# Column mean of an 8192 x 8192 matrix: loads of two rows per partition, a PSUM bank of its own for the last column block, and wider last pieces

## The chip, the cores and the metric

The kernel runs on one core of a Trainium2 chip; the other cores are idle. The metric is the device time of one execution in microseconds (us). The median of three runs of the kernel before is 634.28 us (634.18 to 634.52). "Span" is the time that the profile covers, about 1.8 us less than the device time.

## The reference

```python
def setup_inputs():
    return {"x": np.random.randn(8192, 8192).astype(np.float32)}

def reference(x):
    return np.mean(x, axis=0)
```

The input has 268.4 MB and the output 32 KB. Every input byte is needed once, so the kernel is a stream of loads with a little arithmetic behind it.

## The kernel before

128 rows at a time go into SBUF (the core's buffer for tiles), one row per partition. TensorE sums over the partitions with a constant 128x32 weight of 1/8192. The 16 blocks of 512 columns go to four banks of PSUM (the memory that TensorE accumulates into), four 32-partition quadrants each, and accumulate over all rows.

```python
    banks = [psp.tile([P, F], f32, name=f"bank{b}") for b in range(NB)]   # F = 512, NB = 4
    for ri in range(n_rt - 1):                     # 63 tiles of 128 rows, five buffers
        t = ld.tile([P, N], f32)
        nc.sync.dma_start(out=t[:], in_=x[ri * P:(ri + 1) * P, :])
        for b in range(NB):
            for q in range(4):
                c = (b * 4 + q) * F
                mm(b, q, 0, F, t[:, c:c + F], ri == 0, False)
    # ... the last 128 rows: three pieces of four blocks, then four pieces of
    # 128 columns of each of the last four blocks (runs of 512 bytes)
    for s in range(F // SPL):                      # SPL = 128
        t = lastp.tile([P, 4, SPL], f32, name=f"lasts{s}")
        nc.sync.dma_start(out=t[:], in_=x_v[r0:r0 + P, b, :, s * SPL:(s + 1) * SPL])
        for q in range(4):
            mm(b, q, s * SPL, SPL, t[:, q, :], False, s == F // SPL - 1)
    nc.vector.tensor_copy(out=r[:], in_=banks[b][:])
    nc.scalar.dma_start(out=out_v[b], in_=r[0:128:32, :])
```

Of the kernel before, what the change touches and what calls it, by code (L numbers as in the profile page):

```python
# [1 line left out]

# [4 lines left out]


@with_exitstack
def kernel(  # L10
    ctx: ExitStack,
    tc: tile.TileContext,
    x: bass.AP,
    out: bass.AP,
):







    nc = tc.nc
    f32 = mybir.dt.float32
    M, N = x.shape
    P = nc.NUM_PARTITIONS
    F = 512
    NB = N // (4 * F)
    n_rt = M // P
    SPL = 128  # L30

    ld = ctx.enter_context(tc.tile_pool(name="ld", bufs=5))
    lastp = ctx.enter_context(tc.tile_pool(name="lastp", bufs=1))
    sg = ctx.enter_context(tc.tile_pool(name="sg", bufs=1))
    psp = ctx.enter_context(tc.tile_pool(name="psum", bufs=1, space=bass.MemoryType.PSUM))
    resp = ctx.enter_context(tc.tile_pool(name="res", bufs=1))

    ones = sg.tile([P, 32], f32)
    nc.vector.memset(ones[:], 1.0 / M)  # L39
    banks = [psp.tile([P, F], f32, name=f"bank{b}") for b in range(NB)]  # L40

    def mm(b, q, c0, w, rhs, start, stop):
        nc.tensor.matmul(  # L43
            out=banks[b][32 * q:32 * q + 32, c0:c0 + w],
            lhsT=ones[:],
            rhs=rhs,
            start=start,
            stop=stop,
            tile_position=(0, 32 * q),
            skip_group_check=True,  # L50
        )

    for ri in range(n_rt - 1):
        t = ld.tile([P, N], f32)
        nc.sync.dma_start(out=t[:], in_=x[ri * P:(ri + 1) * P, :])  # L55
        for b in range(NB):
            for q in range(4):
                c = (b * 4 + q) * F
                mm(b, q, 0, F, t[:, c:c + F], ri == 0, False)

    r0 = (n_rt - 1) * P
    out_v = out.rearrange("(b q c) -> b q c", b=NB, q=4)
    x_v = x.rearrange("r (b q c) -> r b q c", b=NB, q=4)
    for b in range(NB - 1):
        t = lastp.tile([P, 4, F], f32, name=f"last{b}")
        nc.sync.dma_start(out=t[:], in_=x_v[r0:r0 + P, b])
        for q in range(4):
            mm(b, q, 0, F, t[:, q, :], False, True)
        r = resp.tile([P, F], f32, name=f"r{b}")
        nc.vector.tensor_copy(out=r[:], in_=banks[b][:])  # L70
        nc.scalar.dma_start(out=out_v[b], in_=r[0:128:32, :])
    b = NB - 1
    r = resp.tile([P, F], f32, name=f"r{b}")
    for s in range(F // SPL):
        t = lastp.tile([P, 4, SPL], f32, name=f"lasts{s}")
        nc.sync.dma_start(out=t[:], in_=x_v[r0:r0 + P, b, :, s * SPL:(s + 1) * SPL])  # L76
        for q in range(4):
            mm(b, q, s * SPL, SPL, t[:, q, :], False, s == F // SPL - 1)
    nc.vector.tensor_copy(out=r[:], in_=banks[b][:])  # L79
    nc.scalar.dma_start(out=out_v[b], in_=r[0:128:32, :])  # L80


# [1 line left out]
_INS = ['x']  # L84
_OUTS = [((8192,), 'float32')]


# [23 lines left out]
```

## Time and profile before

| What | Value |
|---|---|
| Time, median | 634.28 us |
| Span | 632.6 us |
| TensorE busy | 57% |
| Load rate, 100 to 600 us | 431 GB/s |
| Last landing of input data | 628.78 us |
| From there to the end of the span | 3.8 us |

The landing of a tile is seen in the timeline: TensorE's first matmul of a tile starts when the tile has landed. The trace also holds the semaphore updates of each load, 16 for a tile, which I take as one from each of the 16 DMA engines. The matmul at 43.54 us starts 0.04 us after the last of its 16, so the slowest engine sets the landing. These are landings of the kernel before near the start (columns: start us, busy us, engine, line, operation, count, and in brackets the idle time before and what ended it):

```profile
32.47 5.95 PE L43 MATMUL bank<-t,ones 128*32 128x512 f32 x32 [4.38 <-DMA t<-in_x_dram]
43.54 5.54 PE L43 MATMUL bank<-t,ones 128*32 128x512 f32 x32 [5.12 <-DMA t<-in_x_dram]
53.27 5.34 PE L43 MATMUL bank<-t,ones 128*32 128x512 f32 x32 [4.18 <-DMA t<-in_x_dram]
```

The last interval is 9.73 us, the usual one. The one before is 11.07 us. A "step" is from here on an interval between landings that is about 1.0 to 1.5 us longer than the usual one.

### The profile page before, as it was taken

The numbers are of one execution on the slowest core, as the hardware profiler recorded it, in microseconds if no ns is written. First come the engines' busy times: TensorE is split into PE (matmuls) and PEld (weight loads), VectorE is DVE, ScalarE is ACT, GpSimd is POOL, SyncE is SP. The second block draws the span as 40 slices with busy tenths as digits, with TensorE's granted clock in tenths as the row PEclk, the third lists the DMA queues.
The fourth block names the chain that finished last, engine by engine and source line by source line (L and its number), as shares of the span: only waits on it lengthen the run. The fifth ranks groups of instructions, "written<-read, shape, count | busy, mean of one in ns | idle before, by whom it ended". The sixth has DMA issues, their size and how long they took to land.

```text
span 632.6 us, 4331 instructions
## 1 busy us (share of the span) xinstructions
PE 363.6 (57%) x2072; PEld 82.7 (13%) x2072; DVE 2.9 (0%) x5; POOL 0.2 (0%) x4
## 2 busy tenths in 40 slices
PE   1564754656547546565476554655646646556466
PEld 0111111111111111111111111111111101111111
DVE  0000000000000000000000000000000000000001
POOL 0000000000000000000000000000000000000000
PEclk9868668667786686677866778668766686687767
DMA  9999999999999999999999999999999999999996
GB/s 371 433 440 437 432 431 431 428 431 430 431 433 430 431 430 433 431 432 431 430 431 431 428 434 430 431 431 430 433 428 431 431 430 431 432 435 430 431 427 233
DMA packets 11665, 268.74 MB, mean 425 GB/s; under 512 B 1136, under 2 KB 3184, under 8 KB 3200
## 3 DMA queue, kind: packets, MB, share of 16 engines
q1 hardware_dynamic: 11616, 268.44, 99.0%
q8 instruction: 16, 0.26, 0.2%
q10 hardware_dynamic: 32, 0.03, 0.0%
q14 instruction: 1, 0.01, 0.0%
HBM read 268.44 MB, written 0.03 MB: 424 GB/s over the span
## 4 chain that ended last, share of the span: by engine, by line
DMA 87%; PE 11%; SPq 1%; issue 0%; DVE 0%
DMA t<-in_x_dram 86%; PE bank L43 11%; DMA lasts<-in_x_dram 1%; SPq L76 1%; SPq L55 0%; DVE r L79 0%
## 5 line engine op out<-in xcount | busy, mean ns | idle before, releaser
L43 PE MATMUL bank<-t,ones 128*32 128x512 f32 x2016 | 359.8, 880 | 265.1 <-DMA t<-in_x_dram 265.1
L43 PEld LDWEIGHTS bank<-t,ones 128*32 128x32 f32 x2016 | 81.2, 153 | 542.5 <-DMA t<-in_x_dram 310.8
L70 DVE COPY r<-bank 128x512 f32<-128x512 f32 x3 | 2.1, 692 | 625.3 <-PE bank L43 625.3
L43 PE MATMUL bank<-last,ones 128*32 128x512 f32 x24 | 2.7, 592 | 0.0
L43 PE MATMUL bank<-lasts,ones 128*32 128x128 f32 x32 | 1.5, 279 | 0.5 <-DMA lasts<-in_x_dram 0.5
L43 PEld LDWEIGHTS bank<-last,ones 128*32 128x32 f32 x24 | 0.7, 110 | 2.2 <-issue 1.9
L43 PEld LDWEIGHTS bank<-lasts,ones 128*32 128x32 f32 x32 | 0.8, 109 | 1.6 <-DMA lasts<-in_x_dram 1.3
L79 DVE COPY r<-bank 128x512 f32<-128x512 f32 x1 | 0.7, 692 | 1.1 <-PE bank L43 1.1
L95 POOL MEMSET const-bfloat16-1.0<- 128x1 bf16 x1 | 0.1, 102 | 0.0
L95 POOL MEMSET const-uint8-127<- 128x1 uint8 x1 | 0.1, 102 | 0.0
L95 POOL MEMSET const-float32-0.0<- 128x1 f32 x1 | 0.1, 99 | 0.2 <-issue 0.2
L95 POOL MEMSET const-float32-1.0<- 128x1 f32 x1 | 0.1, 99 | 0.0
L39 DVE MEMSET ones<- 128x32 f32 x1 | 0.1, 85 | 0.8 <-PEq L95 0.8
## 6 DMA issues: line engine op xcount, KB each, us to landing
t<-in_x_dram SPq DMA_DIRECT2D x63, 4096.0 KB, 43.1
last<-in_x_dram SPq DMA_DIRECT2D x3, 1024.0 KB, 45.3
lasts<-in_x_dram SPq DMA_DIRECT2D x4, 256.0 KB, 19.1
out_dram<-r ACTq DMA_DIRECT2D x4, 8.0 KB
```

The costliest lines, as they stand in the source:

```text
L39: nc.vector.memset(ones[:], 1.0 / M)
L43: nc.tensor.matmul(out=banks[b][32 * q:32 * q + 32, c0:c0 + w], lhsT=ones[:], rhs=rhs, start=start, stop=stop, tile_position=(0, 32 * q), ...
L70: nc.vector.tensor_copy(out=r[:], in_=banks[b][:])
L76: nc.sync.dma_start(out=t[:], in_=x_v[r0:r0 + P, b, :, s * SPL:(s + 1) * SPL])
L79: nc.vector.tensor_copy(out=r[:], in_=banks[b][:])
L95: nc = _bacc.Bacc("TRN2", target_bir_lowering=False, num_devices=1)
```

## The change

Its intent is to cut the fixed cost of packets with runs twice as long, and to end with fewer and wider pieces, while the last block is spread over four quadrants of its own bank so that its matmuls and its copy stay short.

```diff
+    J = 2
+    NBLK = N // F - 1
+    W = F // 4
+    xt = x.rearrange("(t p j) c -> t p j c", p=P, j=J)
-    ld = ctx.enter_context(tc.tile_pool(name="ld", bufs=5))
+    ld = ctx.enter_context(tc.tile_pool(name="ld", bufs=3))
+    edge = psp.tile([P, W], f32, name="edge")
...
+    def sums(t, j, blocks, first, last):
+        for i in blocks:
+            if i < NBLK:
+                mm(banks[i // 4], i % 4, t[:, j, i * F:(i + 1) * F], first, last)
+            else:
+                for q in range(4):
+                    c = i * F + q * W
+                    mm(edge, q, t[:, j, c:c + W], first, last)
...
+    for ti in range(n_t - 1):
+        t = ld.tile([P, J, N], f32)
+        nc.sync.dma_start(out=t[:], in_=xt[ti])
+        for j in range(J):
+            sums(t, j, range(NBLK + 1), ti == 0 and j == 0, False)
+    t = ld.tile([P, J, N], f32)
+    cuts = [(0, 8), (8, 12), (12, 15), (15, 16)]
... (each piece: load, sums, copy of its banks, store on the scalar queue)
```

## The prediction

> **What bounds the kernel now.** I read the page first: the span, the busy shares, the slices and the chain that ended last.
>
> ```profile
> span 632.6 us, 4331 instructions
> PE 363.6 (57%) x2072; PEld 82.7 (13%) x2072; DVE 2.9 (0%) x5; POOL 0.2 (0%) x4
> ...
> DMA  9999999999999999999999999999999999999996
> ...
> DMA t<-in_x_dram 86%; PE bank L43 11%; DMA lasts<-in_x_dram 1%; SPq L76 1%; SPq L55 0%; DVE r L79 0%
> ```
>
> The DMA engines are full in every slice but the last, and TensorE is idle 43% of the time. The "PE bank L43 11%" in the chain is no TensorE bound: it is the step "a buffer was released, so a load was issued", and each such load then waits some 43 us in the queue behind its predecessors. The kernel is a 268.4 MB load stream with a head and a tail. Next I asked the DMA view for the steady stretch from 100 to 600 us.
>
> ```profile
> DMA packets 7404, 215.58 MB, mean 431 GB/s; under 512 B 818, under 2 KB 818, under 8 KB 818
> ...
> q1 hardware_dynamic: 7390, 215.35, 100.1%
> q8 instruction: 13, 0.21, 0.2%
> ```
>
> 215.35 MB is 6572 packets of 32 KB; the other 818 are 4-byte semaphore writes. 100.1% of 16 engines for 500 us is 8008 us, so a packet with its share of semaphore writes costs 1218 ns. So one row of x is one packet. Queue q8 is TensorE's instruction stream, 16 KB at a time, and it takes turns on the same engines.
>
> Then the end, in the chain in order of time, and the engines' load in the same microseconds (window, us, the busy columns, clock, DMA share, GB/s).
>
> ```profile
> 618.32 3.74 SPq L76
> 622.06 0.04 issue
> 622.10 6.68 DMA lasts<-in_x_dram
> 628.78 0.04 issue
> 628.83 0.47 PE bank L43 x8
> 629.30 0.02 issue
> 629.32 0.69 DVE r L79
> ```
>
> ```profile
> 622.00:624.00 2.00, 2.00 (x12) 0.40 (x8) 0.00 (x0) 0.00 (x0) 0.50 1.06 345
> 625.00:626.00 1.00, 1.00 (x12) 0.24 (x8) 0.16 (x1) 0.00 (x0) 1.00 0.77 221
> 627.00:628.00 1.00, 0.92 (x24) 0.34 (x13) 0.83 (x2) 0.00 (x0) 1.00 0.55 165
> ```
>
> The last landing is at 628.78; matmuls, copy and store take 3.8 us more. Before it the DMA share falls to 0.55: about half of the engines are done while the slow ones finish.
>
> **What the Trainium skill says.** "DMA: Bandwidth & Descriptors", section "Where 436 GB/s comes from": 16 ports x 32 B x 850 MHz, 435.2 GB/s. The packet records of this trace agree. The fastest 32 KB packet took 1213 ns and the fastest 8 KB packet 309 ns; the difference, 904 ns for 24,576 B, is 27.19 GB/s per engine, or 435 GB/s for 16. Same page, "Why small descriptors are slow (HBM only)": a fixed overhead of about 3 cycles per packet. The trace shows a larger one: 309 - 8192/27.19 = 7.7 ns, 6.5 cycles of 850 MHz. The 512 B packets fit (18.8 + 7.7 = 26.5; their median is 27 ns). Same page, "Latency and other measured facts": row pitches at large powers of two slow copies (207 GB/s at 512 KiB pitch, 103 at 4 MiB). The pitch between partitions here goes from 32 to 64 KB; no run here shows harm yet. "TensorE: Matmul & The Clock Gate", Part 1: half clock after an idle window of about 3.4 us, full clock after as long a busy one. The trace agrees: TensorE idles 3.4 to 4.4 us before each tile and then runs at 0.50 from 618 to 624 us, 0.85 us for four 512-wide matmuls, and later 0.43 us.
>
> **The change, part by part.** My working formula for a packet of n bytes is 7.7 ns + n/27.19.
>
> (a) *Two rows per partition.* 63 loads of 4 MB become 31 of 8 MB. If the two rows go as one 64 KB packet, 4 MB on one engine costs 4 x (2410 + 7.7) ns + half a 9 ns semaphore write = 9.676 us; now it is 8 x 1213 + 9 = 9.713 us, and the trace's tiles do land every 9.71 or 9.72 us. That is 0.037 us per 4 MB, over 62 such units 2.3 us. If the descriptor generator cuts the run at 32 KB, only the semaphore writes go: 0.0045 x 62 = 0.3 us. I can't tell which from the trace (its largest packet is 32 KB); I give the whole run 0.6. The mean packet is 5 ns above the fastest; I take that extra as per byte, so unchanged.
>
> (b) *Three buffers of 64 KB for five of 32 KB.* A buffer comes free about 9 to 10 us after its tile lands (twice the present 5 to 6.5 us, less the second half's cold clock). A tile takes 19.4 us to stream, so the next load joins the queue with about 29 us of loads ahead of it (before: 4 x 9.7 - 6 = 33). No starvation, 0 us.
>
> (c) *The last pieces.* At present each engine's last 4 MB is 24 packets of 8 KB (7.4 us) and 128 of 512 B (3.5 us), 10.9 us. The real interval between the last full tile (618.35) and the last landing (628.78) is 10.4. The new last 8 MB is 16 packets each of 16, 8, 6 and 2 KB: 16 x (610 + 309 + 234 + 83) = 19.8 us, against 9.7 + 10.9 = 20.6. So 0.8 us is saved. The stall of 3.74 us at L76 (semaphores shared with earlier loads) goes too, but the slow engines were never idle for it, so I count nothing.
>
> (d) *Edge block.* 128-wide matmuls on four quadrants replace one 512-wide: 19 in place of 16 per row group, so TensorE's instructions grow by some 17%, about 3 more 16 KB fetches of 1.07 us spread over 16 engines: +0.2 us.
>
> (e) *After the last landing.* The third piece (12 matmul records, four groups of 0.43 us = 1.7 us at full clock) starts when it lands, 1.3 us before the fourth, so TensorE reaches the edge 0.4 us late and needs 4 x 0.11 us plus 0.3 us latency: 0.85 us after the landing, where it now needs 0.5. The 96-partition copy (0.69 us, from the 128x512 row) lies in front of the edge copy; that one I estimate at 0.25 us (between the 85 ns of the 128x32 memset and the 692 ns of the 128x512 copy, both on VectorE). So the edge copy ends 1.3 to 1.4 us after landing (now 1.2), then waits for the scalar queue to finish the preceding store (0.52 us each): issue at 1.6. From issue to the end of the span is 632.6 - 630.04 = 2.56 us. Sum 4.2 us against 3.8: +0.4. If TensorE has gone cold in the pauses of 1.5 and 2 us, the third piece takes 3.4 us and the edge 0.85: +2.1 us. I give that 0.25, on average +0.9.
>
> Sum with whole 64 KB packets: -2.3 - 0.8 + 0.2 + 0.9 = -2.0 us, so 632.3. With cut packets: -0.3 - 0.8 + 0.2 + 0.9 = 0.0, so 634.3. Weighted 0.6 to 0.4: 633.1. A second way of counting, by each engine's summed packet time (before: 504 packets of 1217.5 ns and the last pieces, 627 us; after, whole: 623.5; cut: 626), gives 1.5 us more in the change's favour, because it ignores which engine is last. I take half of that: **632.4 us**.
>
> **The rivals.** *The tail governs:* fewer and wider pieces at the end and no half-clock would bring the last landing to the mean engine's finish. For it: the DMA share of 0.55 in the last microseconds. Against: the engines run apart by up to some 3 us, which larger packets don't mend. Time 629.5. *Starvation:* with three tiles in flight the fast engines run out of queued work. For it: issue to landing is 43 us now, 4.4 tiles, and only 3 fit after. Against: (b), in bytes the queue is nearly as deep. If each 8 MB tile lost 0.3 us, the sum would be +9 us: 643. *HBM pattern:* 64 KB pitch makes the engines collide. Against: pitches far above it are needed in the skill's table; with 1% on the stream, 639. *Cold end:* TensorE at half clock after the last landing cancels the stream's gain: 634.
>
> **Range and chances.** The floor is 268.4 MB at 435 GB/s = 617 us plus 3.4 us before the stream's even pace and 4 us of end, 624.5, with 1.8 us between the span and the time, 626. Faster by 2% (621.6) is out of reach but for an error in my reading: 0.01. Slower by 2% (647) needs starvation or collisions: 0.03. Same: 0.96. The range of 629.5 to 635 holds both packet cases and both ends.
>
> **What would show it.** Packets of the load queue: about 4500 if whole (31 x 128 + 1024 + 560 semaphore writes), 8500 if cut. The steady rate: 432.5 to 433 GB/s if whole, 431 if cut. Issue of a tile to its landing near 48 us, no slice of the DMA row under 9 before the last. From the last landing to the end 4.2 us warm or about 6 cold. The prediction is wrong if the DMA share dips in the middle, if a tile takes over 19.5 us, or if the packets' mean extra grows with their size.

## The result, and the profile after

The changed kernel takes 634.02 us (633.98 to 634.33, 4 runs) beside 634.40 us (634.18 to 634.55, 4 runs). The ratio is 0.9995 with a 95% interval of 0.9978 to 1.0013: the same. The gain foretold was 1.9 us; measured it is 0.4. Ratios in this document are the mean time of one kernel's runs over that of the other's of the same rounds, so not quite the ratio of the medians that are quoted. Executions over 1.5% slower than the fastest of the same kernel are left out of the means.

The page of the changed kernel, with the lines that answer to those of before:

```profile
span 632.0 us, 4990 instructions
PE 304.2 (48%) x2432; PEld 99.9 (16%) x2432; DVE 3.0 (0%) x6; POOL 0.2 (0%) x4
...
DMA  9999999999999999999999999999999999999994
...
q1 hardware_dynamic: 5552, 268.44, 98.4%
q8 instruction: 19, 0.31, 0.2%
```

The load queue moved the same bytes in less than half the packets (5552 for 11,616), and the share of engine time fell (98.4% for 99.0%). The instruction queue (q8) has 19 fetches of 16 KB; the kernel before has 16.

The DMA view from 100 to 600 us, the counterpart of the one in the prediction:

```profile
DMA packets 3715, 216.34 MB, mean 433 GB/s; under 512 B 402, under 2 KB 402, under 8 KB 402
...
q1 hardware_dynamic: 3699, 216.07, 99.9%
```

216.07 MB in 3297 data packets (3699 less 402 semaphore writes) is 64 KB a packet: the two rows do go as one, and the trace has 3968 packets of 65,536 bytes. 99.9% of 16 engines for 500 us is 7992 us, so a packet with its share of semaphore writes costs 2424 ns, where two packets of before cost 2 x 1218 = 2436. The stream is faster as predicted: 433 GB/s for 431, and tiles of 8 MB land every 19.35 us, which is 9.675 for 4 MB in place of 9.71.

The landings late in the run, in the timeline of the changed kernel:

```profile
567.41 4.78 PE L47 MATMUL bank<-t,ones 128*32 128x512 f32 x27 [9.14 <-DMA t<-in_x_dram]
588.08 4.69 PE L47 MATMUL bank<-t,ones 128*32 128x512 f32 x27 [11.58 <-DMA t<-in_x_dram]
607.62 5.15 PE L47 MATMUL bank<-t,ones 128*32 128x512 f32 x27 [10.56 <-DMA t<-in_x_dram]
```

The first interval is 20.67 us in place of 19.35: a step of 1.3 us again. There are three such intervals (ending at 62.58, 315.63 and 588.08 us), where the kernel before has two.

The engines' load in the last microseconds of the changed kernel (window, us, the busy columns, clock, DMA share, GB/s):

```profile
622.00:624.00 2.00, 1.59 (x16) 0.42 (x16) 0.00 (x0) 0.00 (x0) 1.00 0.55 222
624.00:625.00 1.00, 0.34 (x4) 0.00 (x0) 0.60 (x1) 0.00 (x0) 1.00 0.52 207
625.00:626.00 1.00, 0.00 (x0) 0.00 (x0) 0.10 (x1) 0.00 (x0) 1.00 0.25 88
626.00:627.00 1.00, 0.94 (x9) 0.33 (x12) 0.00 (x0) 0.00 (x0) 1.00 0.12 45
```

The share of 0.55 is about half of the engines, and in the last microsecond a share of 0.12, two engines of 16, still works. TensorE's clock is 1.00 throughout.

The end of the changed kernel, in the timeline (ACTq is the scalar engine's queue of stores):

```profile
626.06 1.49 PE L47 MATMUL bank<-t,ones 128*32 128x512 f32 x9 [1.73 <-DMA t<-in_x_dram]
627.49 0.93 PE L47 MATMUL edge<-t,ones 128*32 128x128 f32 x15
628.04 0.69 DVE L83 COPY r<-bank 96x512 f32<-96x512 f32 x1 [2.94 <-PE bank L47]
628.64 0.28 DVE L88 COPY redge<-edge 128x128 f32<-128x128 f32 x1
629.59 0.55 ACTq L90 DMA_DIRECT2D out_dram<-redge  x1
```

The third piece lands at 626.02 us. The fourth was issued at 588.05 and landed 39.2 us later, at 627.3. Its matmuls end near 628.4, its copy at 628.92, its store is issued at 629.59, and the span ends at 632.0. From the last landing to the end this is 4.7 us; before it was 3.8.

So the last landing came 1.5 us earlier and the end took 0.9 us longer. That leaves the 0.6 us that the spans differ by.

### The profile page after: what moved, and what is told of

It reads as the page before. It is cut to its first block, busy times and chain, and to the rows that moved or that the text cites. A ratio compares the mean times of both kernels' runs of the same rounds, so it can differ in the third digit from the quotient of the medians.

```text
span 632.0 us, 4990 instructions
## 1 busy us (share of the span) xinstructions
PE 304.2 (48%) x2432; PEld 99.9 (16%) x2432; DVE 3.0 (0%) x6; POOL 0.2 (0%) x4
## 3 DMA queue, kind: packets, MB, share of 16 engines
q1 hardware_dynamic: 5552, 268.44, 98.4%
## 4 chain that ended last, share of the span: by engine, by line
DMA 80%; PE 17%; another core or an unknown queue 2%; SPq 0%; issue 0%; DVE 0%; DVEq 0%
DMA t<-in_x_dram 80%; PE bank L47 15%; PE edge L47 2%; SPq L75 0%; DVE r L83 0%; DVEq L116 0%
## 5 line engine op out<-in xcount | busy, mean ns | idle before, releaser
L47 PE MATMUL bank<-t,ones 128*32 128x512 f32 x1920 | 297.0, 739 | 324.2 <-DMA t<-in_x_dram 324.2
L47 PEld LDWEIGHTS bank<-t,ones 128*32 128x32 f32 x1920 | 85.9, 132 | 489.8 <-DMA t<-in_x_dram 311.7
L47 PE MATMUL edge<-t,ones 128*32 128x128 f32 x512 | 51.5, 279 | 0.0
L47 PEld LDWEIGHTS edge<-t,ones 128*32 128x32 f32 x512 | 23.9, 111 | 38.5 <-issue 38.5
L83 DVE COPY r<-bank 128x512 f32<-128x512 f32 (+1 forms) x4 | 2.8, 690 | 625.1 <-PE bank L47 625.1
## 6 DMA issues: line engine op xcount, KB each, us to landing
t<-in_x_dram SPq DMA_DIRECT2D x1, 512.0 KB, 39.2
```

What stands on the lines that cost most here:

```text
L47: nc.tensor.matmul(out=dst[32 * q:32 * q + 32, :], lhsT=ones[:], rhs=rhs, start=first, stop=last, tile_position=(0, 32 * q), skip_group_ch ...
L83: nc.vector.tensor_copy(out=r[:32 * n, :], in_=banks[b][:32 * n, :])
```

## The experiments

Two questions were open. What did the longer packets bring, and why did the last landing move by only 1.5 us where my sum had 2.9 us? The theory is that longer packets saved 2.1 us, and that the additional instructions took 1.4 us of it back: instruction fetches go through the same DMA engines, and they come in rounds of eight, each of which costs the slowest engine one step. The rival for the first question is that packets bring nothing and only the last pieces do. The rivals for the second are that fetches count by their mean, or not at all.

All outputs are right. "Before" is the kernel before on the same chip in the same rounds. By the limit of 2% every run but e3_fill15 counts as the same as the kernel before; the differences below are small, and the intervals say which of them are clear of noise.

| Run | us | Before, us | Ratio | 95% interval |
|---|---|---|---|---|
| changed kernel | 634.02 | 634.40 | 0.9995 | 0.9978 to 1.0013 |
| e1_pad | 636.25 | 634.30 | 1.0030 | 1.0015 to 1.0045 |
| e2_fill3 | 635.71 | 634.30 | 1.0022 | 1.0007 to 1.0037 |
| e3_fill15 | 658.94 | 634.30 | 1.0376 | 1.0350 to 1.0403 |
| e7_loads64 | 632.21 | 634.30 | 0.9967 | 0.9952 to 0.9982 |
| e3b_fill15t | 637.37 | 634.53 | 1.0046 | 1.0029 to 1.0063 |
| e4_spstore | 633.50 | 634.53 | 0.9985 | 0.9970 to 1.0000 |
| e5_noedge | 633.36 | 634.53 | 0.9983 | 0.9968 to 0.9998 |
| e9_pairsum | 630.90 | 634.53 | 0.9943 | 0.9928 to 0.9958 |
| e10_chain | 635.11 | 634.16 | 1.0015 | 1.0000 to 1.0030 |
| e6_wide | 634.47 | 634.16 | 1.0008 | 0.9991 to 1.0024 |
| e11_chain2 | 631.24 | 634.18 | 0.9951 | 0.9938 to 0.9965 |
| e9_again | 630.94 | 634.18 | 0.9950 | 0.9935 to 0.9964 |

### The changed kernel with packets of 32 KB (e1_pad)

```diff
-        t = ld.tile([P, J, N], f32)
-        nc.sync.dma_start(out=t[:], in_=xt[ti])
+        t = ld.tile([P, J, N + 16], f32)
+        nc.sync.dma_start(out=t[:, :, :N], in_=xt[ti])
... (the last tile is padded alike)
```

> The changed kernel with each of the two row slots of the SBUF tile 64 bytes longer, so that the run is no longer contiguous in SBUF and goes as two 32 KB packets; all else is the same. Theory (fixed cost of 7.7 ns a packet matters): 8 packets of 2418 ns become 16 of 1213 ns in each of 31 tiles, 0.064 us each, so 2.0 us slower than the changed kernel, about 636.0 us. Rival A (larger packets bring nothing; the earlier last landing comes from the wider last pieces): the same as the changed kernel, 634.0 us.

It took 636.25 us, 2.2 us more than the changed kernel. The page's line of the load queue:

```profile
q1 hardware_dynamic: 9520, 268.44, 98.5%
```

That is 3968 packets more, 31 tiles of 128. Each engine has 248 packets more, so the 2.2 us are 9 ns for one packet (an estimate from the two medians); the formula had 7.7. Rival A falls.

### The kernel before with 64 KB loads alone (e7_loads64)

```diff
-    for ri in range(n_rt - 1):
-        t = ld.tile([P, N], f32)
-        nc.sync.dma_start(out=t[:], in_=x[ri * P:(ri + 1) * P, :])
+    for ti in range(n_rt // 2 - 1):
+        t = ld.tile([P, 2, N], f32)            # three buffers
+        nc.sync.dma_start(out=t[:], in_=xt[ti])
... (rows 7936 to 8063 as one load of 4 MB into half a tile; four banks,
...  last 128 rows and pieces as before, in the other half)
```

> The kernel before with loads of 256 rows (64 KB runs, three buffers) and nothing else: its own four banks, its own last 4 MB in the same pieces, 16 fetches. Theory: 2.0 us off the stream, two landing steps of 1.4 us as before, end of 3.8 us as before: about 632.4 us, faster than both. Rival A: 634.4 us. If three buffers hurt: above 635 us.

It took 632.21 us, 2.1 us less than before. The landings have two steps (20.83 us at 62.82, 20.81 us at 373.95), there is no dip in the DMA row, and the last piece lands at 626.4:

```profile
626.42 0.43 PE L42 MATMUL bank<-t,ones 128*32 128x128 f32 x8 [0.29 <-DMA t<-in_x_dram]
```

So the loads of 256 rows are worth 2.1 us, and no cost of three buffers is seen. The other parts of the change, taken together, cost 1.8 us: the changed kernel is at 0.9995 of before and this one at 0.9967, though the two intervals just touch.

### The kernel before with more instructions (e2_fill3, e3_fill15, e3b_fill15t)

```diff
         for b in range(NB):
             for q in range(4):
                 ...
+        for d in range(3):                     # 15 in the other two
+            nc.tensor.matmul(out=spare[32 * (d % 4):32 * (d % 4) + 32, :], lhsT=ones[:],
+                             rhs=ones[:],       # e3b: rhs=t[:, 32 * d:32 * d + 32]
+                             start=True, stop=True, tile_position=(0, 32 * (d % 4)), ...)
```

> The kernel before with 3 extra 32-column matmuls per tile on constants into a spare bank, so that TensorE has about as many instructions as in the changed kernel; no data moves otherwise. Theory (instruction fetches queue on 8 of the 16 DMA engines and each delays its engine by about 1.4 us, so each full round of 8 fetches costs the slowest engine 1.4 us): 19 fetches in place of 16 begin a third round, one more step of 1.4 us in the tiles' landings, about 635.7 us. Rival B (fetches spread, only their mean counts): 3 x 1.07 / 16 = 0.2 us, 634.6 us. Rival C (fetches matter through TensorE's stalls): TensorE is idle over 30 per cent, nothing at all.

It took 635.71 us, 1.4 us more than before, with 19 fetches. Two lines of its page and timeline:

```profile
q8 instruction: 19, 0.31, 0.2%
```

```profile
540.39 5.17 PE L45 MATMUL bank<-t,ones 128*32 128x512 f32 x32 [3.11 <-DMA t<-in_x_dram]
551.44 5.35 PE L45 MATMUL bank<-t,ones 128*32 128x512 f32 x24 [5.88 <-DMA t<-in_x_dram]
```

The interval is 11.05 us in place of 9.71: a third step, late in the run, as in the changed kernel. One flaw: the extra matmuls waited for nothing, so nearly all were run in the first microseconds, and the first fetches fell there. The number of fetches and of steps is what the theory said all the same.

> As the run with 3, but 15 extra matmuls per tile: about 31 fetches. Theory with 8 engines: a fourth round, two steps more than before, +2.7 us, about 637.1 us. Rival with a round of 16 engines: 31 fetches are still the second round, the same as the run with 3 extra. Rival B (mean): 15 x 1.07 / 16 = +1.0 us, 635.4 us.

This one failed as an experiment. It took 658.94 us, because the 945 extra matmuls were all run ahead of the tiles that they should have followed. They held up TensorE's work on the tiles until 89 us, in bursts of 2.04 us with about 4 to 5 us of idle time between them. The buffers filled up and the loads stopped, as the DMA row shows in its fourth to sixth slice:

```profile
DMA  9997629999999999999999999999999999999996
```

> The failed run with 15 extra matmuls again, now with the extra matmuls reading the tile just loaded, so that they can't all run at the start. About 31 fetches. Theory (round of 8 engines, each round one step of 1.4 us in the landings): four steps in place of two, +2.8 us over the kernel before, about 637.1 us. Rival (round of 16): two steps with the second at the 17th fetch, +0 to +1.4. Rival (mean only): +1.0, 635.3 us.

With the extra matmuls tied to their tiles it took 637.37 us, 2.8 us over before. It has 31 fetches and four steps, ending at 33.67, 200.34, 357.28 and 523.96 us; the two lines around the fourth:

```profile
512.83 6.62 PE L45 MATMUL bank<-t,ones 128*32 128x512 f32 x32 [3.08 <-DMA t<-in_x_dram]
523.96 6.17 PE L45 MATMUL bank<-t,ones 128*32 128x512 f32 x32 [4.23 <-DMA t<-in_x_dram]
```

Two extra steps for 15 extra fetches, and one for 3: steps come with every eighth fetch. A round of 16 engines would have given no more than two, the mean +1.0 us. The two steps of the kernel before follow its first and ninth fetch (36.7 and 349.0 us); those of the changed kernel follow the first, the ninth and the seventeenth (46.1, 303.9 and 571.5 us).

The records name no engine, but the 16 semaphore updates of each tile show who is late. They are in the trace file; `prof` does not print them. For the changed kernel:

| Landing, us | Fetches started before it | Within 0.5 us of the first update | 1.6 to 2.0 us behind it | 3.1 to 3.6 us behind | 4.7 to 5.0 us behind |
|---|---|---|---|---|---|
| 41.84 | 0 | 16 | 0 | 0 | 0 |
| 62.54 | 1 | 15 | 1 | 0 | 0 |
| 275.55 | 8 | 8 | 8 | 0 | 0 |
| 315.59 | 9 | 8 | 7 | 1 | 0 |
| 548.01 | 16 | 8 | 0 | 8 | 0 |
| 588.03 | 17 | 8 | 0 | 7 | 1 |
| 627.29, last piece | 19 | 8 | 0 | 6 | 2 |

Each fetch sets one update back, always among the same number, eight of 16. The landing moves when a fetch falls on one that is already the last. So at the end half of the engines are done early, six are two steps late and two are three steps late: this is the DMA share of 0.55 and then 0.12. (The nineteenth fetch started only at 625.3 us; no third update is three steps late.)

### The changed kernel without the edge bank (e5_noedge)

```diff
-    NBLK = N // F - 1
+    NBLK = N // F
... (block 15 goes to bank 3, quadrant 3; bank 3 is copied and stored once, after the last piece)
```

> The changed kernel without the bank of its own for the last block: block 15 goes as one 512-wide matmul to the fourth quadrant of bank 3, as the other blocks do; loads and last pieces as in the changed kernel. TensorE's instructions fall back to those of before. Theory: 16 fetches, two steps in the landings in place of three, last landing 1.35 us earlier, near 625.8; but the last block's four matmul records sit on one quadrant (about 1.7 us where the edge took 0.5), with a full copy and one store after them: about 633.2 us. Rival (the instruction stream is harmless): last landing at 627.2 as in the changed kernel, and the end longer by 1.2 us: 635 us.

It took 633.36 us. It has 16 fetches, and the third step is gone:

```profile
624.62 3.18 PE L46 MATMUL bank<-t,ones 128*32 128x512 f32 x16 [1.81 <-DMA t<-in_x_dram]
```

The third piece lands at 624.6 where it landed at 626.0 in the changed kernel, and the fourth at 625.86 for 627.29: 1.4 us earlier. Its and the fourth piece's matmuls then take 3.2 us, because the last block sits on one quadrant, so half of the gain is lost at the end. This is the direct test on the changed kernel: the edge bank shortens the end and costs a round of fetches over the whole run.

### The last store on another queue (e4_spstore)

```diff
-            nc.scalar.dma_start(out=o, in_=r[0:P:32, :])     # the edge block's store
+            nc.sync.dma_start(out=o, in_=r[0:P:32, :])
```

> The changed kernel with the last store (the edge block) issued from the sync queue in place of the scalar queue; nothing else. Theory (the edge store waits 0.67 us, from the copy's end at 628.92 to its issue at 629.59, behind the store of 6 KB on the same queue): 0.6 to 0.7 us off, about 633.4 us. Rival (the end is set by the landing and the receipt of the stores, which share the DMA engines anyway): no change, 634.0 us.

It took 633.50 us, 0.5 us less than the changed kernel. The store is issued at once after the copy:

```profile
628.72 0.28 DVE L88 COPY redge<-edge 128x128 f32<-128x128 f32 x1
629.02 0.65 SPq L90 DMA_DIRECT2D out_dram<-redge  x1
```

The wait was there and was removed, but its worth is not settled. The profiled spans differ by only 0.2 us (631.8 and 632.0), and the two intervals in the table overlap.

### The wide last pieces alone (e6_wide)

```diff
-    (three pieces of 8 KB runs and four of 512 B runs)
+    cuts = [(0, 8), (8, 12), (12, 16)]        # blocks of the last 128 rows
+    for lo, hi in cuts:
+        nc.sync.dma_start(out=t[:, lo:hi, :], in_=x_l[:, lo:hi, :])
... (then for each piece: matmuls, copy and store of its banks)
```

> The kernel before with its last 4 MB in three wide pieces (8, 4 and 4 blocks of whole rows, packets of 16, 8 and 8 KB) in place of three of 8 KB packets and four of 512 B; loads of 128 rows as before. Theory: each engine's last 4 MB costs 8 x (610 + 309 + 309) = 9.8 us in place of 10.9, so the last landing 1.1 us earlier; the last piece then has 8 records of 512 columns (0.9 us for 0.5): about 0.7 us off, 633.6 us. Rival A (the wide pieces were the whole gain of the change in the last landing, 1.6 us): 633.1 us or less.

A miss: 634.47 us against 634.16, so no gain (0.9991 to 1.0024).

```profile
628.12 1.07 PE L43 MATMUL bank<-last,ones 128*32 128x512 f32 x8 [1.08 <-DMA last<-in_x_dram]
```

Its last landing is at 628.07, 0.7 us earlier than in the kernel before (1.1 was expected), but the last piece of 1 MB then takes 1.1 us of matmuls, and landing to end is 4.5 us. The wide pieces move time from before the last landing to behind it.

### Versions that beat both (e9_pairsum, e9_again, e10_chain, e11_chain2)

If the instruction stream costs 1.4 us for every eight fetches, less of it should pay. In e9 VectorE adds a partition's two rows in place, and TensorE then sums half as many blocks:

```diff
+        for g in range(4):
+            c = slice(g * 4 * F, (g + 1) * 4 * F)
+            nc.vector.tensor_tensor(out=t[:, 0, c], in0=t[:, 0, c], in1=t[:, 1, c], op=add)
+            sums(t, 0, range(4 * g, 4 * g + 4), ti == 0, False)
... (no edge; last bank in slices of 384 and 128 columns of each of its four blocks)
```

> An attempt at a better kernel by the same theory: loads of 256 rows in 64 KB packets; VectorE adds the two rows of a partition in place, TensorE then sums 16 blocks per tile in place of 32, so its instruction stream is halved; no edge block; the last bank's columns come in slices of 384 and 128 of each block, so that four quadrants share the last matmuls. Theory: about 8 fetches, one step in the landings in place of two or three, last landing near 625.0, end 3.9 us after it: about 630.8 us. Rival (instruction stream harmless): as the run with 64 KB loads alone, 632.2 us. If VectorE's adds (an estimated 8.5 us per tile of 19.35, from 692 ns per 512 columns with its fixed part) hold the buffers too long: slower than 634 us.

It took 630.90 us: 0.9943 of before and faster than the changed kernel by 3.1 us. Two lines of its page:

```profile
q8 instruction: 8, 0.13, 0.1%
...
L65 DVE TENSOR_TENSOR t<-t 128x2048 f32<-128x2048 f32 x124 | 275.8, 2286 | 337.1 <-DMA t<-in_x_dram 337.1
```

There are 8 fetches and one step (1.0 us, at 101.3 us), and the last landing is at 625.2. The adds take 4 x 2.29 = 9.1 us of each 19.35.

> The pair-sum kernel once more, on the same chip as the mended running sum, so that the two can be compared: 630.9 us, as in its first run.

The second time it took 630.94 us. One of its five runs (641.64 us, the profiled one) was slow and is left out.

In e10 VectorE keeps the whole running sum, adding the previous tile's sum first, and TensorE works only at the end.

```diff
+                nc.vector.tensor_tensor(out=t[:, 0, c], in0=t[:, 0, c], in1=acc[:, 0, c], op=add)
```

> A second attempt at a better kernel: as the pair-sum run, but VectorE keeps the whole running sum (it adds the previous tile's sum, then the second row, in place), and TensorE sums only over the partitions once at the end. Theory: hardly any instructions to fetch, so no step of 1.4 us in the landings: 1.4 us under the pair-sum run, about 629.5 us. Against: 8 adds of 2.29 us are 18.3 us per tile of 19.35, and a buffer stays held until the next tile's first four adds (9.1 us after its landing), so the next load joins a queue with only 10 us of work ahead; if the engines run dry there, slower than 634 us.

A miss: 635.11 us. Queue q8 has one fetch, but VectorE's last sum came late and TensorE's work after it:

```profile
614.06 8.89 DVE L71 TENSOR_TENSOR t<-t 128x2048 f32<-128x2048 f32 x4
...
623.01 7.08 PE L46 MATMUL bank<-t,ones 128*32 128x512 f32 x78 [0.23 <-DVE t L71]
```

> The running-sum run with its end mended: there VectorE's last adds ended at 623.0 us and TensorE did the final 72 matmul records only after them, until 630.2. Now VectorE's chain stops one tile earlier and TensorE takes the last full tile itself, as in the pair-sum run. Theory: the data landed by 624 to 625.3 us in the failed run too, so with an end of 3.7 us after the last landing about 630.0 us, at most 1 us under the pair-sum run. Rival (buffers held too long in the chain, the engines run dry, not only the end was at fault): 633 us or more.

With the chain stopped one tile earlier it took 631.24 us. So the late end was the fault of e10, but e11 isn't faster than e9: its last landing is at 625.6, no earlier than with eight fetches. Queue q8 has one fetch, but a second instruction queue, q14, has two of 8 KB, at 162.3 and 434.2 us. The next landing after each is late, by 0.8 and 1.0 us; here is the first in the timeline:

```profile
q14 instruction: 2, 0.02, 0.0%
```

```profile
158.16 8.90 DVE L72 TENSOR_TENSOR t<-t 128x2048 f32<-128x2048 f32 x4 [1.65 <-DMA t<-in_x_dram]
178.33 8.90 DVE L72 TENSOR_TENSOR t<-t 128x2048 f32<-128x2048 f32 x4 [2.47 <-DMA t<-in_x_dram]
```

In the semaphore updates both fell on the same engine: the last of the 16 is 0.6 us behind the first, then 1.4, then 2.4. So e11 has as much delay in its landings as e9. The buffers, held longer in the chain, are not to blame: all other intervals of the whole tiles are 19.33 to 19.36 us. Which engine's instructions q14 brings, no record says.

## Why the prediction was right or wrong

The time lay in the range of 629.5 to 635 and the class was right. The point, 632.4, was 1.6 us too low: a gain of 1.9 us was foretold and 0.4 us came. That the range held is in part luck. The 634.0 us measured are what the prediction gives for packets cut at 32 KB (634.3) and for a cold end (634), and neither happened: the packets were whole and the clock was 1.00.

**(a) Right.** Whole 64 KB packets, 2.3 us foretold: 2.1 us with the loads alone (e7_loads64), 2.2 us when they were cut (e1_pad). The parts of its count of packets, 3968 + 1024 + 560, give 5552, which is what the queue has; the "about 4500" is a slip, as is 8500 for cut packets (e1_pad has 9520).

**(b) Right.** No starvation. Issue to landing is 49.0 us, and the intervals between landings are about 19.35 us outside the steps (up to 19.55 in three). One sign of being wrong that the prediction named, a tile of over 19.5 us, did come, with the three steps of about 20.7 us above all; the cause is (d), not starvation.

**(c) About right in size at the landing, but not worth that in time.** 0.8 us foretold; e6_wide landed 0.7 us earlier and gave it back in its longer end. Between e7_loads64 and e5_noedge, which have the same 64 KB loads and 16 fetches, the wider pieces are worth 0.5 us at the landing (626.38 and 625.86).

**(d) The step that failed.** "+0.2 us", from three more fetches "spread over 16 engines". The runs show that fetches are not to be averaged: e2_fill3, with the same number of fetches as the changed kernel, lost 1.4 us, and e5_noedge, with the old number, landed 1.4 us earlier. A landing waits for the slowest engine, and the seventeenth fetch starts a third round on the same eight engines. The evidence was in the profile of before: two intervals of 11.07 and 11.09 us among intervals of 9.71.

**(e) Right in kind, too small when warm.** TensorE stayed at full clock, the case for which +0.4 us was foretold; it became +0.9 (4.7 against 3.8 us). The third piece's matmuls took 1.9 us for 1.7, the edge was done 1.1 us after the landing for 0.85, and the store was issued 2.3 us after it for 1.6, held behind the store on the same queue. From issue to end it took 2.4 us for 2.56. The average of +0.9 over the warm and the cold case is the measured number by luck: no cold case came, and its own weights (0.75 and 0.25 of +0.4 and +2.1) give 0.8.

The accounts at the last landing, from one trace to the next: 628.78 us before, 626.38 with the 64 KB loads alone (e7_loads64), 625.86 with the wide pieces too (e5_noedge), 627.29 with the edge bank too. That is -2.4, -0.5 and +1.4, together -1.5. With +0.9 at the end this is 0.6 us of span. The allowance of half of 1.5 us for the second way of counting was wrong too: that count ignores which engine is last, and this is what decided. Its 1.5 seems to be 3.5 us at the landing (627 to 623.5) less the net sum of 2.0, which has the end's +0.9 in it; against the 2.9 at the landing it is 0.6.

Of the rivals, starvation and the 64 KB pitch did not happen. "The tail governs" named the idle half of the engines, but not its cause.

## What to carry to other kernels

In a stream near the DMA limit a fixed cost of 8 to 9 ns per packet is worth halving, but look at the landings and not at the mean rate: the slowest of the 16 engines sets them. The instructions of a fully unrolled kernel come through the same engines, so a change that adds instructions on an idle engine can cost time in a stream of loads, and one that removes them can gain it. Ask of every wider last piece what it leaves to be done after it has landed.

## What the Trainium skill lacked or had wrong

- "DMA: Bandwidth & Descriptors", section "Why small descriptors are slow (HBM only)", has about 3 cycles of overhead per packet, and 32 bytes of descriptor metadata for each operation; by an estimate from these figures, at 850 MHz and 27.19 bytes per ns, this is 4.7 ns. The packet records here give 7.7 ns, and the two runs that differ in packets alone, e1_pad and the changed kernel, 2.2 us for 248 packets, 9 ns.
- "Trainium Architecture — The Big Picture", section "The software stack", has the instruction streams moved to the engines when the program is loaded. Here 16 KB fetches go on during the run, on the DMA engines that carry the data: 16 for 4331 instructions, 19 for 4990, 31 for 8111, 8 for 2451. Another page, "Runtime: NRT & Kernel Launch", section "Instruction fetch mechanics", has this right: fetches of 16 KiB in the course of the run.
- That section calls the cost of a fetch mostly hidden, and says nothing of what it costs a stream of loads. Here it is one step of 1.0 to 1.5 us in the landings for every eight fetches begun (one step at 8, two at 16, three at 19, four at 31), because they fall on eight of the 16 DMA engines in turn.
